# Weight low parts three chunks ahead and summed from HBM, with another order of the tiles in the recurrent branch

## The chip, the cores and the metric

The kernel runs on one core of one Trainium2 chip, in one launch. The metric is device time in microseconds, from the first to the last instruction of an execution; the number given for a kernel is the median of its runs. Engines are named as in the profile: PE (TensorE), DVE (VectorE), ACT (ScalarE), POOL (GpSimd), SP (SyncE, which here only issues transfers).

## The reference, cut to what matters

512 tokens of width 1024 go through two blocks, all in fp32. The first is a hybrid attention layer; the second is a layer run twice with its own weights (`l` = 0, 1).

```python
def hybrid_layer(x, ...):                    # first block, once
    proj = rms_norm(x) @ w_in                # q, three k/v pairs, gates, z, indexer ...
    kc, vc = compress(k), compress(v)        # silu(flat @ w1 + b1) @ w2 over blocks of 32
    o_nsa = g0 * compressed + g1 * selected + g2 * window      # 8 heads
    score = sum_h relu(qi @ ki) * wi         # indexer; top 128 keys of each query
    o_dsa = attention over the chosen keys   # 8 heads
    return x + concat(o_nsa * silu(z_n), o_dsa * silu(z_d)) @ w_out

def hybrid_layer_2(x, c, positions, ...):    # second block, for l in 0, 1
    mod = c @ w_ada + b_ada                  # 6 vectors: shift, scale, gate, twice
    h = rms_norm(x) * (1 + sc_m) + sh_m
    x_lru, q_down, kv_down, k_rope, gate_a, gate_b = split(h @ w_in)
    y_a = rg_lru(causal_depthwise_conv(x_lru), positions, ...)   # gated linear scan over tokens
    y_b = mla(q_down, kv_down, k_rope, ...)  # 8 heads of latent attention
    x = x + g_m * ((sigmoid(gate_a) * y_a + sigmoid(gate_b) * y_b) @ w_out)
    h = rms_norm(x) * (1 + sc_f) + sh_f
    gate, up = split(h @ w_ffn_in)
    return x + g_f * ((silu(gate) * up) @ w_ffn_out)
# and a last rms_norm
```

## The kernel before

**Products.** Every large product is made of three on TensorE. A weight tile of 128 x up to 1024 (a *chunk*) comes from HBM as `raw`; ACT rounds it to the matmul's format, `wh`; `wl` is what the rounding left over, raw - wh. The activations are split alike into `hh` and `hl`, and the product is hh·wh + hl·wh + hh·wl: 24 matmuls of 512 columns for a chunk. So a chunk can't be finished before its `wl` is there.

**Chunks.** `plan` lists all chunks in the order of their use, each with an engine for its low part. `load_chunk` (L172) issues the load on SP. `split_chunk` (L185) makes `wh` on ACT and then `wl` in one of two ways. With `DV`, DVE subtracts. With `GP`, ACT writes -raw to `wl`, and POOL issues a DMA that adds `raw`, from SBUF, to it (L203; the two together give raw less what the first copy rounded to). `run_ahead` (L211) splits up to `ahead[0]` chunks beyond the one in use, two in most places, and loads a chunk further; `take` (L221) hands a chunk to the code that multiplies. `raw`, `wh` and `wl` are rings of three buffers each. The `raw` of a chunk is free when all that reads it is done, in a GP chunk its accumulating DMA too.

**Order.** Code written as generators runs beside the matmuls: `go` starts one, `tick` and `pe` step all of them as matmuls are issued, `finish` runs one to its end. So the place of an evacuation or a split among the instructions of its engine follows from how much matmul work was written before it. `order(...)` names the engines that keep the written order strictly.

**Stages.** Times are of the profiled execution. *Projections* (6 to 206 us): the groups E, kv, C, A, Bq, Dv and z of `w_in`; beside C and A stand the compress steps (`cmp_step`), whose weights `cw1` are chunks of the plan too; `post_scores` and `best_keys` make the indexer's scores and, by rounds of MAX8 and MATCH_REPLACE8 on DVE, the mask of the top keys. *Attention* (216 to 366): units of 128 queries; beside them `ada_first(8)` makes a part of layer 0's `mod` from 16 tiles `ada` of 256 KB, one DVE product each. *First output* (366 to 418): eight chunks of `wo1`; `ada_first(0)` with 16 more tiles stands here. *Entry* of a layer (`enter`): norm and the first two input tiles; it also sums `shift` times the raw weights on DVE (`shifts`), which is why these chunks keep `raw` longer. *Branch* (layer 0: 440 to 612): four chunks of the latent vectors `lat`, then eight input tiles (conv, gates by `small_gates` on the split conv output `xch`/`xcl`, scan in `recur`), eight `gate_a` tiles and eight `gate_b` tiles, with `uqr` and `uqk`, the query weights of the latent attention. *Latent attention* `mla`, *wo2*, *feed-forward* (`ffi`, `ffo`; layer 0: 745 to 1100), then the same for layer 1, and the output. The 160 `ada` tiles of layer 0's other vectors and of layer 1 are loaded beside all this (L1859) and multiplied on DVE.

The branch before goes by pairs: gate_a, small gates, gate_a, scan, two gate_b, then the next pair's two input tiles. The first head of `mla` begins at the last pair's gate_b tiles, behind that pair's `recur`.

## Time and profile before

| | us |
|---|---|
| median of 3 runs | 1773.9 (1771.15 to 1777.37) |
| profiled execution, time | 1770.8 |
| profiled execution, span | 1769.0 |
| PE busy | 1687.9 (95%) |
| DVE busy | 1103.6 (62%) |
| ACT busy | 958.2 (54%) |
| POOL busy | 381.1 (22%) |
| granted TensorE clock, mean | 0.986 |
| DMA | 235.91 MB, 133 GB/s |

The share of an engine is a mean over stages with different limits. TensorE's row is the one to start from: what it isn't busy, and what it is busy at a lower clock, is all that can be won without leaving matmuls out. For every other engine a busy share matters only where TensorE's waits name it.

### The profile page before, as it was taken

How to read it: one execution, taken by the hardware profiler on the slowest of the kernel's cores; microseconds unless marked ns; L12 is line 12 of the kernel's file. 1: busy time of each engine (PE TensorE's matmuls, PEld its weight loads, DVE VectorE, ACT ScalarE, POOL GpSimd, SP SyncE). 2: the span in 40 equal slices, each digit the busy share in tenths (PEclk: the TensorE clock that was granted, in tenths of full speed). 3: DMA queues.
4: the chain of work that ended last, by engine and by line, in shares of the span. 5: the costliest groups of instructions: out<-in, count | busy, mean ns of one | idle time of the engine just before them, and what ended most of it. 6: DMA issues, size and time to landing. Idle time of an engine off the chain costs nothing.

```text
span 1769.0 us, 22764 instructions
## 1 busy us (share of the span) xinstructions
PE 1687.9 (95%) x8122; PEld 1389.5 (79%) x8124; DVE 1103.6 (62%) x2048; ACT 958.2 (54%) x1729; POOL 381.1 (22%) x429
## 2 busy tenths in 40 slices
PE   6979899989998999999999999999999999999998
PEld 5868677667776788888888888887788888888887
DVE  5767788768689876746555546657676733333335
ACT  5558787975766786442222224887885532222223
POOL 3236344531225244100000000235243100000000
PEclk9989999999999999999999999999999999999999
DMA  6546643165787822366457443564422343333322
GB/s 199 148 125 140 150 108 84 48 177 134 189 256 209 236 49 70 98 184 226 155 190 236 149 132 94 146 146 126 124 60 72 97 129 96 96 95 98 100 86 74
DMA packets 84976, 235.91 MB, mean 133 GB/s; under 512 B 10368, under 2 KB 13056, under 8 KB 84864
## 3 DMA queue, kind: packets, MB, share of 16 engines
q1 hardware_dynamic: 73600, 194.82, 35.5%
q0 software_dynamic: 11264, 39.65, 12.1%
q8 instruction: 64, 1.05, 0.2%
q14 instruction: 48, 0.39, 0.1%
HBM read 192.69 MB, written 2.10 MB: 110 GB/s over the span
## 4 chain that ended last, share of the span: by engine, by line
PE 65%; DVE 10%; issue 9%; DMA 8%; ACT 6%; POOL 3%; SPq 0%; POOLq 0%; DVEq 0%; ACTq 0%
PE mm L84 38%; PE s L84 20%; PE o L84 3%; DMA wl<-raw 3%; DMA ada<-in_ada_dram 3%; DVE ada L1850 2%; DMA raw<-in_w_dram 2%; PE pt L930 1%; ACT p L71 1%; PE pt L2017 1%; PE pt L84 1%; DVE wl L74 1%; DVE xc L1534 1%; ACT L71 1%; DVE xl L1622 0%
## 5 line engine op out<-in xcount | busy, mean ns | idle before, releaser
L71 ACT ACTIVATE wh<-raw 128x1024 fp32r<-128x1024 f32 (+3 forms) x257 | 263.3, 1026 | 578.6 <-PE mm L84 361.7
L84 PE MATMUL mm<-hh,wh 128*128 128x512 f32 x1408 | 444.9, 393 | 3.6 <-DVE z L74 3.4
L84 PEld LDWEIGHTS mm<-hh,wh 128*128 128x128 f32 x1408 | 265.3, 189 | 58.4 <-DVE z L74 3.5
L84 PE MATMUL mm<-hh,wl 128*128 128x512 f32 x736 | 290.1, 394 | 4.6 <-DMA wl<-raw 4.5
L74 DVE TENSOR_TENSOR wl<-raw,wh 128x1024 fp32r<-128x1024 f32 (+3 forms) x179 | 213.8, 1196 | 115.9 <-ACT wh L71 113.5
L84 PE MATMUL s<-hh,wh 128*128 128x512 f32 x688 | 213.8, 390 | 0.0
L74 POOL TENSOR_TENSOR nv<-nv,pwr 128x4 f32<-128x4 f32 (+1 forms) x6 | 7.4, 1234 | 776.7 <-DVE nv L1321 432.7
L84 PEld LDWEIGHTS mm<-hh,wl 128*128 128x128 f32 x736 | 139.4, 189 | 35.3 <-DMA wl<-raw 6.5
L84 PEld LDWEIGHTS s<-hh,wh 128*128 128x128 f32 x688 | 129.4, 188 | 26.6
L84 PE MATMUL s<-hh,wl 128*128 128x512 f32 x352 | 137.8, 392 | 2.7 <-DMA wl<-raw 2.7
L84 PE MATMUL mm<-uh,wh 128*128 128x512 f32 (+1 forms) x364 | 139.2, 382 | 0.0
L84 PE MATMUL mm<-ul,wh 128*128 128x512 f32 (+1 forms) x364 | 139.0, 382 | 0.0
L84 PE MATMUL mm<-uh,wl 128*128 128x512 f32 (+1 forms) x364 | 139.0, 382 | 0.0
L203 POOL DMA_DIRECT2D wl<-raw x78 | 68.9, 887 | 254.4 <-ACT wl L71 214.8
L1850 DVE SCALAR_TENSOR_TENSOR ada<-ada,c_bc 128x512 f32<-128x512 f32 x160 | 115.8, 756 | 7.2 <-DMA ada<-in_ada_dram 7.2
L74 DVE TENSOR_TENSOR sg<-s,sg 128x512 f32<-128x512 f32 x42 | 29.1, 692 | 116.4 <-PE s L84 116.4
L71 ACT ACTIVATE p<-s,st 128x512 f32<-128x512 f32 (+3 forms) x160 | 83.9, 527 | 23.7 <-DVE st L1994 16.9
L1769 DVE SCALAR_TENSOR_TENSOR x<-mm,mod,x 128x512 f32<-128x512 f32 x46 | 34.5, 751 | 92.2 <-PE mm L84 92.2
L84 PEld LDWEIGHTS s<-hh,wl 128*128 128x128 f32 x352 | 66.4, 189 | 17.7 <-DMA wl<-raw 4.0
L84 PE MATMUL mm<-yh,wh 128*128 128x512 f32 x256 | 79.6, 392 | 0.3 <-DVE x L2119 0.3
L71 ACT ACTIVATE wl<-raw 128x1024 fp32r<-128x1024 f32 (+3 forms) x78 | 79.9, 1024 | 0.0
L84 PEld LDWEIGHTS mm<-uh,wl 128*128 128x128 f32 x364 | 68.4, 188 | 13.3
(430 smaller groups left out, 3640.7 us busy)
## 6 DMA issues: line engine op xcount, KB each, us to landing
ada<-in_ada_dram SPq DMA_DIRECT2D x192, 256.0 KB, 4.1
raw<-in_ffi_dram SPq DMA_DIRECT2D x88, 512.0 KB, 3.6
wl<-raw POOLq DMA_DIRECT2D x67, 512.0 KB, 5.4
raw<-in_w_dram SPq DMA_DIRECT2D x66, 512.0 KB, 3.9
raw<-in_ffo_dram SPq DMA_DIRECT2D x32, 512.0 KB, 3.7
raw<-in_wo_dram SPq DMA_DIRECT2D x24, 512.0 KB, 3.7
raw<-in_ffo_dram SPq DMA_DIRECT2D x16, 384.0 KB, 3.2
x<-in_xT_dram SPq DMA_DIRECT2D x16, 256.0 KB, 4.9
```

Of the source, the lines that this page charges most:

```text
L71: nc.scalar.activation(o, i, f, **kw)
L74: (e or nc.vector).tensor_tensor(o, x, y, op)
L84: nc.tensor.matmul(o, l, r, start=start, stop=stop)
L203: nc.gpsimd.dma_start(lo[:, :n].bitcast(F32), raw[:, :n], accum_op=ALU.add)
L930: nc.tensor.transpose(tp[:n, r * 128:(r + 1) * 128], srcs[r], ident)
L1534: nc.vector.scalar_tensor_tensor(xc[:, d:], x_[:, :S - d], vec[:, j * 8 + m:j * 8 + m + 1], xc[:, d:], ALU.mult, ALU.add)
L1769: nc.vector.scalar_tensor_tensor(x[m], ps, mod[:, 40 + m:41 + m], x[m], ALU.mult, ALU.add)
L1850: nc.vector.scalar_tensor_tensor(w, w, 1.0, c_bc[:, hf * 512:(hf + 1) * 512], ALU.mult, ALU.mult, accum_out=parts[l][:, j, hf:hf + 1])
L2017: nc.tensor.transpose(tp[:, kb * 128:(kb + 1) * 128], p[:, kb * 128:(kb + 1) * 128], ident)
```

## The change

- *Splitting.* `split_chunk` becomes `low_first` and `high`. `low_first` makes ACT's -raw and issues the accumulation, three chunks ahead (`ahead` 3); `high` makes `wh` two chunks ahead; loads go four ahead. The accumulating DMA reads the chunk from HBM again instead of from `raw`. The rings are now `raw` 2, `wh` 3, `wl` 4.
- *Who makes the low part.* More chunks are GP: the accumulating DMAs grow from 78 to 125, the 1024-wide DVE subtractions shrink from 153 to 111. All of C, A, Bq, Dv, the branch, `uqr`, `uqk`, `wo2` and the first five `ffi` chunks are GP; two E chunks are subtracted on POOL; the other `ffi` chunks and `ffo` stay on DVE.
- *Compress weights.* `cw1` leaves the plan; `load_cw` puts it into two tiles of the `ada` ring, half a step each, after the step before has been issued.
- *Shift sums.* The sums of `shifts` move from `enter` into `low_first`.
- *Branch order.* A table `STEPS` sets it: the next pair's input tiles (X) come before the gate_b tiles (B), and the first head's projections (L) before the last scan (R6).
- *Modulation.* `ada_both` runs `ada_first(8)` and `ada_first(0)` beside the attention.
- *End of the projections.* The stage ends when the mask of the third group of queries exists; the fourth is finished by the first unit that needs it. Its scores lie in a tile of their own.
- *Small ones.* x loads of the start are contiguous, E's third chunk is loaded behind them; the tile `isres` goes (the test stands in the operation that used it); ten attention tiles `p` become nine. ACT's table loads grow from 45 to 57.

```diff
-    def split_chunk(i):
+    def low_first(i):
+        n, e = plan[i][3:]
+        while count[0] <= i:
+            load_chunk()
+        raw = loaded[i]
+        if e is GP:
+            lo = lows[i] = wpool.tile([128, 1024], F32R, tag="wl", name=name("wl"), bufs=LB)
+            act(lo[:, :n], raw[:, :n], scale=-1.0)
+            yield 1
+            nc.gpsimd.dma_start(lo[:, :n], source(i), accum_op=ALU.add)
...
-            nc.gpsimd.dma_start(lo[:, :n].bitcast(F32), raw[:, :n], accum_op=ALU.add)
...
+    def high(i):
...
+        if e is GP:
+            ready[i] = h, lows.pop(i), raw
+            act(h[:, :n], raw[:, :n])
             return
...
-    ahead = [2]
+    ahead = [3]
...
-        while count[1] <= min(i + ahead[0], len(plan) - 1):
-            k = count[1]
+        end = len(plan) - 1
+        while count[3] <= min(i + ahead[0] - 1, end):
+            k = count[3]
+            if count[1] <= k:
+                count[1] += 1
+                yield from low_first(k)
+            count[3] += 1
+            yield from high(k)
+        while count[1] <= min(i + ahead[0], end):
             count[1] += 1
-            yield from split_chunk(k)
-        if count[0] <= i + 3:
+            yield from low_first(count[1] - 1)
+        while count[0] <= min(i + ahead[0] + 1, end):
             load_chunk()
...
+    STEPS = [(s_[0], int(s_[1])) for s_ in """
+        A0 S0 S1 A1 R0 X2 X3 B0 T0 B1
+        A2 S2 S3 A3 R2 X4 X5 B2 Q0 B3
+        A4 S4 S5 A5 R4 X6 X7 B4 B5
+        A6 S6 S7 A7 L0 R6 B6 B7
+        """.split()]
...
-    while procs:
+    while any(p not in keys_p for p in procs):
         tick()
+    while 2 not in masks:
+        step(keys_p[0])
...
-    zs, more, ad = z_steps(), after_first(), ada_first(8)
+    def ada_both():
+        yield from ada_first(8)
+        yield from ada_first(0)
+
+    zs, more, ad = z_steps(), after_first(), ada_both()
```

On ACT, in layer 0's branch, this is the stretch from the first pair's last operations to the second pair's conv output. `gb` is a gate_b tile, `xl` and `xc` are an input tile and its conv, `xch` its high part, `wh`/`wl` the two copies of a chunk. Before:

```order
L71 ACTIVATE gb_4953<-mm 128x512
L71 ACTIVATE wh_4959<-raw_4921 128x1024
L71 ACTIVATE wl_4960<-raw_4921 128x1024
L71 ACT_TABLE_LOAD
L71 ACTIVATE gb_4900<-gb_4900 128x512
L71 ACTIVATE xl_4993<-mm 128x512
L71 ACTIVATE wh_5004<-raw_4967 128x1024
L71 ACTIVATE xc_4995<-xl_4993,vec_3910 128x512
L71 ACTIVATE wl_5005<-raw_4967 128x1024
L71 ACTIVATE gb_4953<-gb_4953 128x512
L71 ACTIVATE wh_5053<-raw_5013 128x1024
L71 ACTIVATE xch_5029<-xc_4995 128x512
```

And after the change:

```order
L74 ACTIVATE wh_4898<-raw_4808 128x1024
L74 ACTIVATE xc_4890<-xl_4888,vec_3982 128x512
L74 ACTIVATE wl_4900<-raw_4854 128x1024
L74 ACT_TABLE_LOAD
L74 ACTIVATE ri_4777<-ri_4777 128x512
L74 ACTIVATE ri_4791<-ri_4791 128x512
L74 ACTIVATE xl_4947<-mm 128x512
L74 ACTIVATE wh_4958<-raw_4854 128x1024
L74 ACTIVATE xc_4949<-xl_4947,vec_3982 128x512
L74 ACTIVATE wl_4960<-raw_4909 128x1024
L74 ACTIVATE xch_4931<-xc_4890 128x512
L74 ACTIVATE gb_4999<-mm 128x512
```

The input tiles and their convs now stand ahead of both gate_b tiles, and the two copies of a chunk have parted: `wl` of a chunk stands a tile ahead of its own `wh`.

On DVE, around the first head of `mla` in layer 0: `qkl` are the low parts of the first head's k and q, which its scores need; `ri` and the scan that writes `xl` belong to the last pair's `recur`. Before:

```order
L1611 SCALAR_TENSOR_TENSOR ri_5840<-a_5936,ri_5840 128x512
L74 TENSOR_TENSOR ri_5840<-ri_5840,isres 128x512
L1850 SCALAR_TENSOR_TENSOR ada_5906,part<-ada_5906,c_bc 128x512
L1850 SCALAR_TENSOR_TENSOR ada_5974,part<-ada_5974,c_bc 128x512
L1968 SCALAR_TENSOR_TENSOR qkl_5978<-s,qkh_5977 128x512
L1850 SCALAR_TENSOR_TENSOR ada_6002,part<-ada_6002,c_bc 128x512
L77 TENSOR_TENSOR qkl_5986<-s,qkh_5985 128x512
```

And after the change:

```order
L2011 SCALAR_TENSOR_TENSOR qkl_5956<-s,qkh_5955 128x512
L1893 SCALAR_TENSOR_TENSOR ada_5903,part<-ada_5903,c_bc 128x512
L80 TENSOR_TENSOR qkl_5964<-s,qkh_5963 128x512
L1893 SCALAR_TENSOR_TENSOR ada_5915,part<-ada_5915,c_bc 128x512
L1893 SCALAR_TENSOR_TENSOR ada_5943,part<-ada_5943,c_bc 128x512
L1656 SCALAR_TENSOR_TENSOR ri_5859<-a_5984,ri_5859 128x512
L1657 SCALAR_TENSOR_TENSOR ri_5859<-nres,ri_5859 128x512
```

The head's two low parts moved ahead of the whole of the last `recur`; products of modulation tiles still stand between them.

On SP, the loads around the end of the attention: `raw` of `in_wo` are the chunks of the first output, `ada` the modulation tiles, `x` the residual. Before:

```order
L179 DMA raw_3937<-in_wo_dram 128x1024
L284 DMA x_3900<-in_xT_dram 128x512 x4
L179 DMA raw_3968<-in_wo_dram 128x1024
L1183 DMA posi<-in_pos_dram 128x4
L1185 DMA posr<-in_posr_dram 128x512
L1187 DMA invf<-in_invf_dram 128x32
L1189 DMA vec_3910<-in_vec_dram 128x67
L1189 DMA vec_3911<-in_vec_dram 128x67
L1190 DMA fgain<-in_fgain_dram 128x8
L1064 DMA ada_3943<-in_ada_dram 128x512
L1064 DMA ada_3951<-in_ada_dram 128x512
L284 DMA x_3990<-in_xT_dram 128x512 x3
```

And after the change:

```order
L1126 DMA ada_3851<-in_ada_dram 128x512
L1509 DMA gw_4533<-in_lwa_dram 128x512
L1509 DMA gw_4599<-in_lwx_dram 128x512
L1248 DMA posi<-in_pos_dram 128x4
L1250 DMA posr<-in_posr_dram 128x512
L1252 DMA invf<-in_invf_dram 128x32
L1254 DMA vec_3982<-in_vec_dram 128x67
L1254 DMA vec_3983<-in_vec_dram 128x67
L1255 DMA fgain<-in_fgain_dram 128x8
L321 DMA x_4045<-in_xT_dram 128x512 x4
L194 DMA raw_4013<-in_wo_dram 128x1024
L194 DMA raw_4036<-in_wo_dram 128x1024
```

All modulation tiles of `ada_first` are now loaded before the tables, and between them and the following chunks of `wo` no more of them stand.

## Rows read from the trace of the kernel before

**Rows 1.** The page: busy time and share of TensorE, with its count of instructions

```profile
PE 1687.9 (95%) x8122; PEld 1389.5 (79%) x8124; DVE 1103.6 (62%) x2048; ACT 958.2 (54%) x1729; POOL 381.1 (22%) x429
```

**Rows 2.** Waits of TensorE: line, what it waited for, us in total, times, longest

```profile
PE mm L84 <- DMA wl<-raw: 24.0, 10, 4.8
...
PE pt L513 <- ACT R L71: 6.2, 2, 5.0
PE s L84 <- ACT xch L71: 4.0, 2, 3.0
PE pt L84 <- DMA wl<-raw: 3.7, 1, 3.7
PE s L84 <- DVE qkl L77: 3.6, 1, 3.6
PE mm L84 <- DVE z L74: 3.4, 1, 3.4
PE s L84 <- DMA wl<-raw: 2.7, 3, 1.3
PE pt L1648 <- DVE lat L1500: 2.2, 2, 1.2
...
PE s L84 <- DVE xcl L77: 1.7, 2, 1.6
PE pt L2017 <- POOL p L2000: 1.7, 1, 1.7
```

**Rows 3.** Windows: length, busy PE, PEld, DVE, ACT, POOL, clock, DMA share, GB/s

```profile
17.50:20.90 3.40, 3.22 (x12) 3.22 (x13) 3.09 (x5) 1.88 (x4) 3.07 (x3) 0.53 0.62 186
...
sum 23.80, PE 21.17 PEld 17.69 DVE 18.98 ACT 14.14 POOL 9.74; mean PE 3.53 PEld 2.95 DVE 3.16 ACT 2.36 POOL 1.62
...
195.00:201.80 6.80, 6.21 (x15) 4.91 (x16) 6.59 (x14) 1.55 (x3) 0.86 (x1) 0.51 1.01 217
611.50:618.30 6.80, 6.14 (x17) 4.71 (x18) 5.43 (x10) 3.69 (x6) 0.86 (x1) 0.52 0.83 205
```

**Rows 4.** The same view by stage: projections' end, attention, layer 0's branch, feed-forward

```profile
140.00:206.00 66.00, 60.16 (x289) 49.72 (x288) 58.69 (x111) 53.68 (x144) 35.45 (x41) 0.95 0.65 151
216.00:366.00 150.00, 144.26 (x835) 106.28 (x836) 119.59 (x282) 126.18 (x323) 73.46 (x99) 1.00 0.29 73
...
440.00:612.00 172.00, 156.12 (x677) 126.90 (x677) 138.31 (x243) 122.75 (x181) 57.11 (x46) 0.98 0.77 220
...
800.00:1090.00 290.00, 290.00 (x1281) 240.23 (x1280) 164.03 (x304) 79.94 (x99) 0.00 (x0) 1.00 0.55 174
```

**Rows 5.** Groups by shape: count | busy us, mean ns of one | idle before, releaser

```profile
L71 ACT ACTIVATE wh<-raw 128x1024 fp32r<-128x1024 f32 x220 | 232.3, 1058 | 530.6 <-PE mm L84 340.4 <-issue 138.7 <-PE s L84 26.7
L74 DVE TENSOR_TENSOR wl<-raw,wh 128x1024 fp32r<-128x1024 f32 x153 | 189.5, 1239 | 109.6 <-ACT wh L71 107.3
...
L71 ACT ACTIVATE wl<-raw 128x1024 fp32r<-128x1024 f32 x67 | 70.4, 1051 | 0.0
...
L71 ACT ACT_TABLE_LOAD x45 | 57.7, 1283 | 1.5 <-PEq L2254 0.7
...
L1058 DVE SCALAR_TENSOR_TENSOR ada<-ada,c_bc 128x512 f32<-128x512 f32 x32 | 22.9, 719 | 15.1 <-DMA ada<-in_ada_dram 15.0
```

**Rows 6.** The page: DMA queue (packets, MB, share) and issues (KB, us to landing)

```profile
q0 software_dynamic: 11264, 39.65, 12.1%
...
raw<-in_ffi_dram SPq DMA_DIRECT2D x88, 512.0 KB, 3.6
wl<-raw POOLq DMA_DIRECT2D x67, 512.0 KB, 5.4
```

**Rows 7.** Timeline of POOL in layer 0's branch: start, us, instruction

```profile
558.33 0.88 POOL L203 DMA_DIRECT2D wl<-raw  x1
```

**Rows 8.** Timeline of DVE at the end of the projections

```profile
194.13 0.68 DVE L602 MATCH_REPLACE8 sco<-m,sco 128x512 f32<-128x512 f32 x1
194.84 0.69 DVE L74 TENSOR_TENSOR z<-mm,rbx 128x512 f32<-128x512 f32 x1
```

More of the change, by code (lines that the diff above doesn't have):

```diff
@@ L30 @@
 AR = 4
+RB = 2
+HB = 3
+LB = 4
 TICK = 640.0
@@ L166, in wait, with shifts, source @@
             yield 1
-    plan = []
-    loaded, ready, count = {}, {}, [0, 0, 0]
+    plan, shift_of, shift_parts = [], {}, {}
+    loaded, lows, ready, count = {}, {}, {}, [0, 0, 0, 0]
+    def shifts(l, c0, i):
+        if i == 0:
+            shift_parts[l, c0] = pp.tile([128, 3, 128], F32, tag="wsh", name=name("wsh"), bufs=1)
+        return shift_parts[l, c0][:, i], mods[l][:, c0:c0 + 8]
+    def source(i):
+        key, l, o, n, _ = plan[i]
+        return (a[key] if l is None else a[key][l])[:, o:o + n]
     def load_chunk(beside=None):
@@ L183, in load_chunk @@
             count[0] += 1
-    def split_chunk(i):
+    def low_first(i):
[8 more added lines that the diff above has]
+            nc.gpsimd.dma_start(lo[:, :n], source(i), accum_op=ALU.add)
+            if i in shift_of:
+                by_k, shift = shifts(*shift_of[i])
+                for kt in range(KD):
+                    w_ = raw[:, kt * 128:(kt + 1) * 128]
+                    if kt == 0:
+                        nc.vector.tensor_scalar(by_k, w_, shift[:, 0:1], None, ALU.mult)
+                    else:
+                        nc.vector.scalar_tensor_tensor(by_k, w_, shift[:, kt:kt + 1], by_k, ALU.mult, ALU.add)
+                    if kt % 2:
+                        yield 1
@@ L1327, in rms, with enter @@
         yield rb
-    def enter(st, gain, shift, weights, pool):
+    def enter(st, gain, shift, part, weights, pool):
         hs, box = [], {"n": 0}
@@ L1381, in enter @@
         sh = pp.tile([128, 3], F32, tag="shw", name=name("shw"), bufs=2)
-        by_k = Lp.tile([128, 3, 128], F32, "F", name("wsh"))
-        def shifts(i):
-            for kt in range(KD):
-                raw = ws[i][2][:, kt * 128:(kt + 1) * 128]
-                if kt == 0:
-                    nc.vector.tensor_scalar(by_k[:, i], raw, shift[:, 0:1], None, ALU.mult)
-                else:
-                    nc.vector.scalar_tensor_tensor(by_k[:, i], raw, shift[:, kt:kt + 1], by_k[:, i], ALU.mult, ALU.add)
-                if kt % 2:
-                    yield 1
         def last(k):
@@ L1400, in enter @@
         for i in range(2):
-            ahead[0] = 2 - i
+            ahead[0] = 3
             ws.append(take(*weights[i]))
-            parts_.append(go(later(5, shifts(i))))
             w_dense(xg, ws[i], pss[i], 0, KD - 1, need=last)
@@ L1715, in layer @@
         order(mybir.EngineType.PE, mybir.EngineType.Activation)
-        hs, first, need = enter(st, sc1[:, 8:16], mod[:, 24:32], [("ffi", l, k * 1024, 1024) for k in range(3)], POOL_FF)
+        hs, first, need = enter(st, sc1[:, 8:16], mod[:, 24:32], (l, 24), [("ffi", l, k * 1024, 1024) for k in range(3)], POOL_FF)
         if l == 0:
@@ L2062, in mla @@
         yield
-        ahead[0] = 1
+        ahead[0] = 2
         yy = {}
```

200 lines of the change are left out of this document (97 added, 103 removed).

## The prediction, made before the changed kernel was run

> **What bounds the kernel now.** I read the page's busy times first: TensorE works 95% of the span [rows 1], so only TensorE's own lost time counts, and a busy DVE, ACT or DMA counts where TensorE waits for it. The view of waits on TensorE says what that lost time is [rows 2]. Three of its rows are waits for a low part, `wl<-raw`, still on its way through DMA: 24.0 + 3.7 + 2.7 = 30.4 us in 14 waits. Next come `R`, which the change leaves as it is, then `xch`, `xcl` and `lat` (the recurrent branch, 4.0 + 1.7 + 2.2), `qkl` and `p` (the first latent-attention head, 3.6 + 1.7) and `z` (end of the projections, 3.4). Then the granted clock: behind each of the longer waits TensorE runs at its 1.2 GHz level, half of 2.4, for 3.4 or 6.8 us. Six such stretches stand behind a wait for a low part and sum to 23.8 us (the first, at 17.5 us, with a clock of 0.53); one of 6.8 us stands behind `z`, one behind `qkl` [rows 3]. In the feed-forward part nothing is lost: 290.00 busy of 290 us, 1281 matmuls, so 0.226 us for each and 24 x 0.226 = 5.4 us for a weight chunk [rows 4]. What the change does there can cost but not gain.
>
> **What it removes.**
>
> A. Low parts. Today the low part of chunk n is begun two chunks before its use: an ACT copy of 1.05 us [rows 5], the issue on POOL of 0.88 us [rows 7], a landing of 5.4 us [rows 6], 7.3 us in all against 2 x 5.4 = 10.9 us of lead. That holds until something stands ahead of it. The row at 558.33 us is such a case: POOL issues a low part only when a run of products has ended, the last of them at 558.33 [rows 7], and one of the 14 waits follows. With three chunks of lead there are 16.3 us, so a delay up to 9 us is hidden instead of up to 3.6. No single wait of the 14 is above 4.8 us [rows 2], so nearly all should go. I take 27 of 30.4; ends 15 and 30.4.
>
> B. The clock behind those waits. 23.8 us at about half rate lose about 11.5 us of matmuls. If the waits go, so do these; I take 10.5, ends 5 and 11.5.
>
> C. Order in the branch. The next pair's input tiles now come before the gate tiles, so between a conv's input and the matmuls that read `xch` and `xcl` there are two more tiles, 11 us. The 5.7 us of those waits go, and the transposes of `lat` stand behind a gate tile (2.2). I take 7.5; ends 4 and 7.9.
>
> D. First head. Its projections now stand ahead of the last scan's gate tiles; two tiles, 11 us, lie between them and the scores, where one lay. 3.6 (`qkl`) + 1.7 (`p`) + 6.8 us at half rate = 3.3: 8.6. I take 8.5; ends 3 and 8.6.
>
> E. End of the projections. TensorE waits 3.4 us for `z`, which on DVE stands behind three rounds of the top-k search (the row of `z` at 194.84 follows one of their steps directly [rows 8]), and then loses 3.4 to the clock. The change ends this stage without waiting for the last search, but the order on DVE still has rounds ahead of each `z`, and DVE is busy 58.69 of these 66 us [rows 4]. So I take only 2; ends 0 and 6.8.
>
> Sum of the gains: 27 + 10.5 + 7.5 + 8.5 + 2 = 55.5 us.
>
> **What it adds.**
>
> F. The attention stage gets the first layer's 16 modulation products as well as those it had: 16 x 0.72 = 11.5 us of DVE [rows 5]. DVE works 119.59 of the 150 us there, TensorE 144.26 [rows 4]. 131 of 150 still fits, but softmax steps wait behind single products. Ends 0 and 11.5; I take 3, nearer to the lower end, since DVE has 30 us free there and TensorE only 6.
>
> G. DMA in the first layer's branch. More chunks there go the way over ACT and an accumulating DMA: two latent chunks, two gate-a and eight gate-b tiles, and one chunk each of `uqr` and `uqk`, 14 together. The software queue took 12.1% of 16 engines' 1769 us for 39.65 MB [rows 6], that is 214 us over 39.65/0.524 = 75.7 chunks, 2.83 us of all engines for one. The stage's share is 0.77 of 172 us, 132 us [rows 4]; with 14 x 2.83 = 40 it is 172, and the stage itself shall shrink from 172 to about 151 by A to D. So by this price the DMA engines are full there. Lower end 0: an accumulation that reads HBM may take less engine time than one that reads and writes SBUF, and its low parts have 9 us of slack. Upper end 172 - 151 = 21. I take 6, nearer to the lower end, because the share that a queue shows includes time in which its packets wait on one another.
>
> A rule of the Trainium skill stands against the new source: "DMA: Bandwidth & Descriptors", section "Where 436 GB/s comes from", has HBM to SBUF limited at about 358 GB/s and SBUF to SBUF at 435. By that figure the stage's 220 GB/s x 172 us = 37.8 MB plus 14 x 0.524 MB are 45.2 MB, an estimated 126 us, less than 151: G would be 0 and the sum 6 us lower. The row of the stage, a share of 0.77 at 220 GB/s, implies 286 GB/s when full, below the page's figure. No run here shows yet which holds for an accumulation from HBM.
>
> H. Start and compress. The third E chunk's load goes behind all x tiles (0 to 3 us). The compress weights leave the stream of chunks and are loaded into two small tiles just after the step before has read them: eight steps, each with a landing of 3.6 to 5.4 us [rows 6] against a chunk of 5.4 us, so 0 to about 1 us each. Together 0 to 11; I take 4, nearer the lower end as a compress step itself lasts over a microsecond and lies between.
>
> I. ACT. 47 more low copies at 1.05 and 12 more table loads at 1.28 us [rows 5] are 49 + 15 = 65 us. In the branch of the first layer that is some 22 us on 122.75 of 172 [rows 4]; ACT is then at 145 of 151 and becomes the next to be late. DVE loses 42 subtractions of 1.24 us [rows 5]. I take 2; ends 0 and 10.
>
> Nothing for the rest. Two raw buffers instead of three: in the feed-forward part a raw tile is held for its load (3.6), ACT's copy (1.06) and DVE's subtraction (1.24) [rows 5, 6], 5.9 us, and two buffers give 10.9 us for that. What hides it is 5 us of slack; if loads took 8 us there, each chunk would cost TensorE time. The shift sums (16 and 24 DVE operations for a layer's two entries) are only moved earlier. The accumulate needs the raw tile no longer, so a load waits for ACT's two copies alone.
>
> Sum of the costs: 3 + 6 + 4 + 2 = 15 us. Net 40.5. The profiled execution took 1770.8 us; 1770.8 - 40.5 = 1730.3, and the median of the runs stands 3.1 above that execution, so **1733 us**. With all gains at their upper end (65) and no cost it is 1709.
>
> **The rivals.**
>
> 1. The DMA engines are full in the first layer's branch. For it: the 172 us of G, and a DVE wait for modulation data there. Against it: layer two's branch has no such load, and the packets of an accumulate may overlap. It costs 21 in place of 6, and the low parts of this stage are late again (another 0 to 10): 1748 to 1762, with 1750 as its likeliest.
>
> 2. The change does not do what it says. The low parts are late because of POOL's queue and ACT's, not because they are begun late, and both queues get more work: 47 more issues on POOL. Then A and B bring nothing (37.5): 1770. For it is the row at 558.33 us; against it that the delay seen there is below the added lead.
>
> 3. Slower. An accumulation from HBM, with the loads of raw, wh and the modulation tiles on the same engines, lands later than three chunks can cover. With a ring of four and three in preparation, a chunk takes at least a third of landing L plus copy, issue and queueing (1.05 + 0.88 + about 1.5 = 3.4), so its wait is (L + 3.4)/3 - 5.4. About 80 chunks before the feed-forward parts go this way. The net gain of 40.5 us is used up at 0.5 us for each, and the kernel is measurably slower from 0.6: L = 3 x 6.0 - 3.4 = 14.6 us, where the landing from SBUF is 5.4 [rows 6]. At L = 16 each waits 1.07 us, +85: 1818 before other waits are hidden in it, about 1790 if half of them are.
>
> **How the numbers follow.** Forecast 0.63 (1712 to 1747), rival 1 0.20, rival 2 0.08, rival 3 0.09. To the low side the range reaches 1712, almost all gains at their ends; to the high side it takes in rival 1, to 1765. What is left out is rivals 2 and 3 and a little of the forecast, 0.2. A run of this kernel can tell 0.3%, 5.3 us, from no change. Faster by more than that (below 1768.6): forecast, rival 1 and a third of rival 2, 0.86. Within: most of the rest of rival 2, 0.05. Slower: rival 3, 0.09.
>
> **What would show it.** Right: no row of TensorE waiting for `wl` above 1 us between 60 and 620 us, and no stretch at half clock there (A, B); no waits for `xch`, `xcl`, `qkl` (C, D); the feed-forward stages still at full busy time. F would show as waits for softmax tiles in the attention, G as a DMA share near 1.0 in the first branch with late `wl` or raw, H as waits for `cw`, I as waits for an ACT result. The landing of the accumulates settles rival 3: below 10 us it is out. The forecast is wrong if new waits on TensorE take more than 15 us, or if the half-clock stretches stay although the waits shrink.

## The result and the profile after

The changed kernel takes 1787.1 us (median of 6 runs, 1782.23 to 1789.53) against 1771.8 us for the kernel before in 6 runs beside it: a ratio of 1.0081, 95% interval 1.0061 to 1.0101. It is slower by 0.8%; the forecast was 1733 us. The profiled execution of the changed kernel has a span of 1786.5 us, 17.5 more than before.

The page of the changed kernel: busy times, the queue of the accumulating DMAs (packets, MB, share), and two rows of issues (KB each, us to landing). They answer to [rows 1] and [rows 6].

```profile
PE 1696.1 (95%) x8124; PEld 1396.0 (78%) x8124; DVE 1049.1 (59%) x1998; ACT 1017.1 (57%) x1788; POOL 410.3 (23%) x478
...
q0 software_dynamic: 18032, 63.98, 21.3%
...
wl<-in_w_dram POOLq DMA_DIRECT2D x65, 512.0 KB, 6.6
...
wl<-in_wo_dram POOLq DMA_DIRECT2D x24, 512.0 KB, 6.8
```

TensorE's idle time is 90.4 us where it was 81.1, and its busy time is 8.2 us longer for the same matmuls, most of which is time at the lower clock (0.983 on the mean against 0.986). The low parts land 6.6 us after their issue instead of 5.4. The waits of TensorE (line, releaser, us in total, times, longest), to be laid beside [rows 2]:

```profile
PE s L87 <- ACT p L74: 8.9, 8, 4.0
PE mm L87 <- DMA wl<-in_w_dram: 7.2, 4, 2.7
...
PE mm L87 <- ACT gb L74: 6.2, 2, 3.5
PE pt L1693 <- DVE cl L1706: 5.7, 1, 5.7
PE mm L87 <- ACT ga L74: 5.5, 1, 5.5
...
PE o L87 <- DMA cw<-in_cw_dram: 3.1, 2, 1.7
PE s L87 <- ACT qkh L74: 2.9, 1, 2.9
...
PE mm L87 <- DMA wl<-in_wo_dram: 2.0, 1, 2.0
```

The waits for low parts did go: 7.2 + 2.0 and a last 0.5 instead of 30.4. `xch`, `xcl` and `z` are gone too. In their place stand results of ACT (`gb`, `ga`, `qkh`, `p`) and `cl`.

Where the time went is read from the timeline of TensorE, at the first matmul of each stage. "Sum" is the sum of squares `o<-ones,sa` at a layer's entry; a head starts at `s<-qkh,qkh`.

| stage | before, us | after, us | change |
|---|---|---|---|
| start to the first product of `ptl` with VA (projections) | 226.4 | 209.4 | -17.0 |
| attention, to first product of `wo1` | 142.0 | 156.5 | +14.5 |
| first output, to the first sum | 48.1 | 43.6 | -4.5 |
| layer 0: entry and branch, to the first head | 191.6 | 196.8 | +5.2 |
| layer 0: heads, to `wo2` | 73.5 | 85.0 | +11.5 |
| layer 0: `wo2`, to the second sum | 57.1 | 59.1 | +2.0 |
| layer 0: feed-forward, to the third sum | 362.5 | 364.6 | +2.1 |
| layer 1: entry to the fourth sum | 296.5 | 300.7 | +4.2 |
| layer 1: feed-forward and output | the same within 0.4 | | |

The projections are 17.0 us shorter (other executions of the same code there took 224.5 to 228.1 before and 205.3 to 209.4 after); seven of the 14 waits for low parts, 15.9 us, lay there. The attention gave most of it back: of its 14.5 us 8.5 are idle time of TensorE and 6.0 the same matmuls at a lower clock (0.97 on the mean against 1.00). Layer 0 from the first to the second sum, where A to D were to save some 20 us, grew from 322.2 to 340.9. The windows of that stage in the changed kernel (branch, then first heads; columns as in [rows 3]):

```profile
440.00:605.00 165.00, 145.25 (x626) 116.86 (x625) 108.72 (x209) 118.76 (x171) 54.30 (x51) 0.98 0.92 249
605.00:700.00 95.00, 81.19 (x482) 69.11 (x481) 68.65 (x157) 72.13 (x155) 37.91 (x53) 0.91 0.36 86
```

The DMA share of the branch rose from 0.77 to 0.92, and the heads behind it run at a mean clock of 0.91. What ACT and DVE waited for between the first two sums of the changed kernel:

```profile
ACT wl L74 <- DMA raw<-in_w_dram: 26.5, 10, 5.5
...
ACT wl L74 <- DMA raw<-in_uqk_dram: 7.5, 3, 4.7
```

```profile
DVE ada L1893 <- DMA ada<-in_ada_dram: 30.1, 12, 5.6
```

With the chunks of `wo` and `ffi` ACT's waits for raw make 40 us. Before, ACT waited 3.1 us for raw there and DVE 7.2 us for modulation tiles:

```profile
ACT wh L71 <- DMA raw<-in_w_dram: 3.1, 2, 2.0
```

```profile
DVE ada L1850 <- DMA ada<-in_ada_dram: 7.2, 5, 3.1
```

SP issues both kinds of load in one order, and it too stands longer at the modulation tiles, until DVE has freed a buffer for the next one, with the loads of raw behind it (the changed kernel, then the one before):

```profile
SPq L1902 <- DVE ada L1893: 92.1, 33, 8.2
```

```profile
SPq L1859 <- DVE ada L1850: 51.7, 34, 5.0
```

How this reaches TensorE shows in a stretch of the timeline (start, us, instruction, idle before and its releaser):

```profile
550.44 1.06 ACT L74 ACTIVATE wl<-raw 128x1024 fp32r<-128x1024 f32 x1 [3.12 <-DMA raw<-in_w_dram]
...
553.07 1.28 ACT L74 ACT_TABLE_LOAD   x1 [1.57 <-DVE ada L1893]
...
556.85 1.28 ACT L74 ACT_TABLE_LOAD   x1
...
558.14 0.60 ACT L74 ACTIVATE ga<-mm 128x512 f32<-128x512 f32 x1
...
558.79 1.22 PE L87 MATMUL mm<-hh,wh 128*128 128x512 f32 x2 [5.52 <-ACT ga L74]
```

ACT stands 3.12 us at the early copy for a low part, because its raw has not landed; then it waits for DVE, which is busy with modulation products; the evacuation of a gate tile comes behind all that, and TensorE needs the buffer that this tile leaves. The early copy, made to take the low part out of TensorE's way, now stands in ACT's.

### The profile page after: what moved, and what is told of

Read it like the earlier page. It is cut to its first block, busy times and chain, and to the rows that moved or that the text cites. A ratio compares the mean times of both kernels' runs of the same rounds, so it can differ in the third digit from the quotient of the medians.

```text
span 1786.5 us, 22790 instructions
## 1 busy us (share of the span) xinstructions
PE 1696.1 (95%) x8124; PEld 1396.0 (78%) x8124; DVE 1049.1 (59%) x1998; ACT 1017.1 (57%) x1788; POOL 410.3 (23%) x478
## 4 chain that ended last, share of the span: by engine, by line
PE 68%; DMA 8%; DVE 7%; ACT 6%; issue 6%; POOL 3%; SPq 0%; DVEq 0%; POOLq 0%; ACTq 0%
PE mm L87 42%; PE s L87 19%; PE o L87 3%; DMA ada<-in_ada_dram 3%; DMA raw<-in_w_dram 3%; DMA raw<-in_ffi_dram 1%; PE pt L992 1%; PE pt L2060 1%; DVE ada L1893 1%; ACT R L74 1%; ACT wl L74 1%; ACT wh L74 1%; DVE xc L1579 1%; PE pt L87 1%; DMA wl<-in_wo_dram 1%
## 5 line engine op out<-in xcount | busy, mean ns | idle before, releaser
L77 DVE TENSOR_TENSOR wl<-raw,wh 128x1024 fp32r<-128x1024 f32 (+2 forms) x130 | 152.7, 1175 | 114.1 <-ACT wh L74 111.8
L209 POOL DMA_DIRECT2D wl<-in_w_dram x81 | 71.1, 884 | 592.2 <-DVE wsh L217 331.4
L74 ACT ACTIVATE wl<-raw 128x1024 fp32r<-128x1024 f32 (+2 forms) x125 | 129.6, 1036 | 79.7 <-DMA raw<-in_w_dram 41.3
L1893 DVE SCALAR_TENSOR_TENSOR ada<-ada,c_bc 128x512 f32<-128x512 f32 x160 | 115.8, 755 | 30.4 <-DMA ada<-in_ada_dram 30.1
L74 ACT ACTIVATE p<-s,st 128x512 f32<-128x512 f32 (+3 forms) x160 | 84.0, 528 | 21.3 <-DVE st L2037 12.1
L87 PEld LDWEIGHTS mm<-uh,wh 128*128 128x128 f32 x364 | 68.4, 188 | 13.3
L87 PEld LDWEIGHTS mm<-ul,wh 128*128 128x128 f32 x364 | 68.4, 188 | 13.3
```

Source lines behind the costliest of these rows:

```text
L74: nc.scalar.activation(o, i, f, **kw)
L77: (e or nc.vector).tensor_tensor(o, x, y, op)
L87: nc.tensor.matmul(o, l, r, start=start, stop=stop)
L209: nc.gpsimd.dma_start(lo[:, :n], source(i), accum_op=ALU.add)
L1893: nc.vector.scalar_tensor_tensor(w, w, 1.0, c_bc[:, hf * 512:(hf + 1) * 512], ALU.mult, ALU.mult, accum_out=parts[l][:, j, hf:hf + 1])
```

## Experiments

Unless said otherwise the measure is the stage from the first to the second sum: 322.2 us before, 340.9 in the changed kernel. Ratios are to the kernel before, with 95% intervals. A stage is read from one execution: kernels with the same code there took 322.2 to 322.9 us with the old code and 340.8 to 345.3 with the changed one, so a few us between two kernels say little.

**Is it the number of accumulations?** Fourteen chunks of a branch go back to DVE:

```diff
-                w2_(16 + m)
+                w2_(16 + m, DV)
...
-                chunks("uqr", l, 0, 1024, 1, GP)
+                chunks("uqr", l, 0, 1024, 1, DV)
```

(and likewise two latent chunks, two gate_a tiles and the first `uqk` chunk.)

> The changed kernel with one thing undone: in both layers' branches the low parts of two latent chunks, two gate_a and eight gate_b tiles, uqr and the first uqk chunk are subtracted on DVE again, as before the change. Measure: layer 0's stage from the row sum of squares (o<-ones,sa) ahead of it to the next one, 322.3 us before the change, 340.9 after. Theory 1 (the DMA engines are full, share 0.92; raw comes late, and ACT, whose -raw copy stands first in its order, holds everything behind it): 14 accumulations fewer are some 40 us of engine time, so the share falls to about 0.75, ACT's waits for raw in the branch from 33 to under 10 us, and the stage to 325 or less; the whole kernel gains 12 to 18 us. Theory 2 (two raw buffers are too few): the loads still wait for ACT's second copy, the stage stays above 335. Theory 3 (the new order of tiles): above 335 too.

Measured: 1787.1 us, 1.0086 (1.0063 to 1.0110), no gain; the stage takes 336.4. Its DMA share fell, from 0.69 over the stage of the changed kernel to 0.57, about that of the kernel before (0.56), yet ACT still waits 29.6 us for raw and DVE 28.0 us for modulation tiles, and TensorE now waits for DVE's own low parts:

```profile
PE mm L87 <- DVE wl L77: 11.5, 3, 5.2
```

So a full set of DMA engines, as rival 1 had it, isn't the whole cause. How much it is of it this run can't tell, because these new waits may hide what the lighter traffic gave.

**Is it the order of tiles?** The old order in the changed kernel (but for the first head's projections, L0, half of which stood ahead of B6 before):

```diff
-        A0 S0 S1 A1 R0 X2 X3 B0 T0 B1
-        A2 S2 S3 A3 R2 X4 X5 B2 Q0 B3
-        A4 S4 S5 A5 R4 X6 X7 B4 B5
-        A6 S6 S7 A7 L0 R6 B6 B7
+        A0 S0 S1 A1 T0 R0 B0 B1 X2 X3
+        A2 S2 S3 A3 R2 B2 B3 X4 X5 Q0
+        A4 S4 S5 A5 R4 B4 X6 X7 B5
+        A6 S6 S7 A7 R6 B6 L0 B7
```

> The changed kernel with the old order of the tiles in the branch (gate_b tiles of a pair ahead of the next pair's input tiles, first head behind the last scan) and all else as changed. Theory 3 (the new order costs): the stage from sum to sum falls from 340.9 towards 325, the total by 10 to 18 us. Theory 1 (DMA full) and theory 2 (two raw buffers): the share stays near 0.92, ACT still waits 25 us or more for raw in the branch, and the stage stays at 335 to 350; it may be longer by the waits for xch, xcl and qkl (up to 15 us) which the order was to remove.

Measured: 1791.3 us, 1.0108 (1.0079 to 1.0136); the stage takes 342.3. The branch to the first head is 212.7 instead of 196.8, the heads 70.7 instead of 85.0. The new order moves some 15 us of waiting from the branch into the heads. In layer 1, which has no modulation loads beside its branch, the old order is the slower one: 307.3 from entry to the fourth sum, where the kernels with the new order and the same code take 298.8 to 304.1.

**The modulation tiles.** 64 tiles of 256 KB are loaded beside layer 0's branch on the same SP queue as raw. Four kernels leave out all or a part of that. Without loads and products, in the changed kernel and in the one before (the sums that the products would make are set to zero once, so that part of `mod` is left out):

```diff
         for j in range(j0, j1):
             for hf in range(2):
+                if l == 0:
+                    yield every
+                    continue
```

> The changed kernel without the 64 modulation tiles of layer 0 that are loaded and multiplied beside its branch (16.8 MB and some 48 us of DVE; that part of mod stays as it is after its bias). Theory 1: 16.8 MB fewer take the DMA share in the branch from 0.92 to about 0.65, ACT's waits for raw from 33 to under 8 us, the stage from 340.9 to 322 or less, total 15 to 22 us less. Theory 2: raw still waits for a free buffer; ACT's waits stay above 20 us and the stage above 332. Theory 3: the same as theory 2, but DVE's own waits for modulation data (30 us) go, which may give up to 8 us.

> The kernel before without the same 64 modulation tiles, as the base for the run above. All theories: its stage of 322.3 us has only one long low-part wait and one DVE wait that come from DMA, so it gains 3 to 10 us; theory 1 wants the gain clearly smaller here than in the changed kernel, theories 2 and 3 want about the same in both.

Then the products without the loads (here the products are of `c` with itself):

```diff
-            nc.vector.scalar_tensor_tensor(w, w, 1.0, c_bc[:, hf * 512:(hf + 1) * 512], ALU.mult, ALU.mult,
+            ch = c_bc[:, hf * 512:(hf + 1) * 512]
+            nc.vector.scalar_tensor_tensor(w, w if l else ch, 1.0, ch, ALU.mult, ALU.mult,
...
-                nc.sync.dma_start(w, a["ada"][l, :, j * D + hf * 512:j * D + (hf + 1) * 512])
+                if l:
+                    nc.sync.dma_start(w, a["ada"][l, :, j * D + hf * 512:j * D + (hf + 1) * 512])
```

And loads and products without the dependence: the loads stay, and the product neither reads nor writes the loaded tile (`sp_` is a tile of its own):

```diff
-            nc.vector.scalar_tensor_tensor(w, w, 1.0, c_bc[:, hf * 512:(hf + 1) * 512], ALU.mult, ALU.mult,
+            ch = c_bc[:, hf * 512:(hf + 1) * 512]
+            nc.vector.scalar_tensor_tensor(w if l else sp_, w if l else ch, 1.0, ch, ALU.mult, ALU.mult,
```

> The changed kernel without the 64 loads of modulation tiles beside layer 0's branch, but with their 64 DVE products (each of c with itself, so that part of mod is other data). The kernel without both had a stage of 302.5 us between the first two sums of squares, the changed kernel 340.9. Theory A (the late tiles: DVE, in order, stands at a product whose tile has not landed, and holds conv, xcl, qkl and the softmax sums behind it; or their loads take the engines): stage 303 to 312. Theory B (the 48 us of DVE time themselves): 325 to 340.

> The changed kernel with the same 64 loads and the same 64 products, but the products no longer read the tiles that were loaded (they are of c with itself), so the traffic stays and DVE never waits for it. If the in-order wait on DVE is what costs, the stage falls from 340.9 to 305 to 318, with a DMA share near 0.9. If the traffic itself (engines full, raw and low parts late) is, it stays above 330 though DVE waits for no tile.

| kernel | total, us | stage, us |
|---|---|---|
| changed | 1787.1 | 340.9 |
| changed, products don't read the loaded tiles | 1781.3 | 331.7 |
| changed, no loads | 1761.5 | 312.0 |
| changed, neither loads nor products | 1745.4 | 302.5 |
| before | 1771.8 | 322.2 |
| before, neither loads nor products | 1754.4 | 304.4 |

The stage in the three kernels that leave something out of the changed one, in that order (columns as in [rows 3]):

```profile
404.90:736.60 331.70, 303.24 (x1472) 251.20 (x1471) 225.42 (x448) 234.89 (x389) 110.20 (x122) 0.97 0.70 179
```

```profile
405.50:717.50 312.00, 297.21 (x1472) 248.57 (x1472) 226.03 (x448) 236.82 (x391) 113.98 (x122) 0.99 0.62 137
```

```profile
406.10:708.60 302.50, 293.39 (x1472) 246.01 (x1472) 173.96 (x317) 234.92 (x390) 111.27 (x122) 1.00 0.61 141
```

The 64 tiles cost the changed kernel 38.4 us (340.9 - 302.5), the kernel before only 17.8 (322.2 - 304.4). Of the 38.4, 9.2 go when DVE no longer stands in order behind a tile that has not landed, 19.7 more when the loads are gone, and 9.5 with the products. The first of these is the least certain: the profiled execution was the fastest of that kernel's seven, and by the medians of the whole kernels the three steps are 5.8, 19.9 and 16.0. Without the tiles the changed branch is as good as the old one, 302.5 against 304.4. So the change and these loads hinder each other, and about half of the cost is the loads being there at all: raw in this stage lands after a median of 5.7 us in the changed kernel, 3.9 before, and 4.5 in the changed kernel without the loads. Whether that is the engines' bandwidth or the place in SP's one queue isn't told apart by these runs.

The old kernel without the tiles shows something else. These are the longest waits of its TensorE in the stage:

```profile
PE pt L84 <- DMA wl<-raw: 2.8, 1, 2.8
PE pt L1649 <- DVE lat L1501: 2.1, 2, 1.2
PE mm L84 <- DMA wl<-raw: 1.3, 1, 1.3
PE s L84 <- ACT p L71: 1.1, 1, 1.1
```

The waits for `xch`, `xcl` and `qkl` [rows 2], 9.3 us, are gone here, though the order of tiles is the old one. They were a cost of the modulation tiles, not of the order alone.

**Two raw buffers.** Three of them, paid for by smaller rings elsewhere (in the attention too, so that only layer 0 counts; the ring R of the second block shrinks as well, and layer 1, which has it too, takes 300.3 against 300.7):

```diff
-RB = 2
+RB = 3
...
-    P = HP(pP, {"R": 3, "cp": 4})
+    P = HP(pP, {"R": 2, "cp": 3})
...
-           {"p": 9, "pth": 3, "ptl": 3, "pc": 2, "st": 5})
+           {"p": 7, "pth": 3, "ptl": 3, "pc": 2, "st": 5})
...
-    Lp = HP(ctx.enter_context(tc.tile_pool(name="block2", bufs=1, reuse_waits="tile")), {"R": 20, "PT": 4, "G": 16, "F": FB, "qr": 1})
+    Lp = HP(ctx.enter_context(tc.tile_pool(name="block2", bufs=1, reuse_waits="tile")), {"R": 18, "PT": 4, "G": 16, "F": FB, "qr": 1})
```

> The changed kernel with three raw buffers instead of two; the room comes from smaller rings elsewhere (R 3 to 2 and cp 4 to 3 in the projections, p 9 to 7 in the attention, R 20 to 18 in the second block), so only the branch of layer 0 is to be compared. The last runs put theory 1 (DMA engines full) in doubt: with a share of 0.67 the modulation tiles were as late as with 0.92. Theory 2, now with its size: with two buffers a load may start only when ACT has made wh of the chunk two before, and on ACT the next low copy follows one chunk (5.4 us) later, while copy and landing take 1 + 5 us; so ACT waits at that copy, and SP, waiting for the buffer, holds the modulation tiles queued behind the load. With three buffers ACT's waits for raw in the stage between the first two sums of squares (340.9 us) fall from 40 to under 10 us, DVE's for modulation data from 30 to under 12, and the stage to 315 to 325. Theory 1: the share stays near 0.9 and so do the waits; stage above 335.

Measured: the stage takes 340.0, though ACT's waits for raw fell from 40 us to 4.4, and DVE's for modulation tiles grew from 30.1 to 41.1:

```profile
ACT wl L74 <- DMA raw<-in_w_dram: 4.4, 2, 4.2
```

```profile
DVE ada L1893 <- DMA ada<-in_ada_dram: 41.1, 13, 8.5
```

The wait moved to DVE and the modulation tiles, and TensorE lost as much as ever. (1802.3 us in total, most of the added time in the attention, 175.9 us with seven p tiles.)

**The source of the accumulation.** Two chunks of lead for the low part and one for wh, rings of three, once from HBM and once from SBUF, all else as changed (the edit from one to the other; its `.bitcast(F32)` on the target was not tried apart, here and in the next run):

```diff
-            nc.gpsimd.dma_start(lo[:, :n], source(i), accum_op=ALU.add)
+            nc.gpsimd.dma_start(lo[:, :n].bitcast(F32), raw[:, :n], accum_op=ALU.add)
```

> The changed kernel with low parts two chunks ahead, wh one ahead, loads three ahead and rings of three raw, three wh and three wl (the early places of ahead as before the change); source of the accumulation, order and engines as changed. Theory 2 (two raw buffers): the stage between the first two sums of squares falls from 340.9 to 320 to 330, ACT's waits for raw there under 15 us, while waits of TensorE for wl come back in the projections (10 to 20 us). Theory 1 (DMA full): same traffic, so the stage stays above 335.

> The run a_two with one difference: the accumulating DMA reads the chunk from SBUF (raw) again instead of from HBM. If the source matters (theory 1, HBM traffic), the landing of wl falls from 6.6 to about 5.4 us, the DMA share in layer 0's branch falls by 0.05 or more, and the stage is at least 8 us shorter than in a_two. If it doesn't, the stage differs by less than 5 us; raw is held longer by the landing, so it may even be longer.

Measured: 1808.9 us (1.0194, 1.0169 to 1.0220) from HBM, 1784.8 (1.0058, 1.0040 to 1.0077) from SBUF: 24 us. Not in the stage, where it was looked for and where they differ by 2.7 the other way (336.3 and 339.0), but up to the first sum (397.6 and 389.3) and behind the second. The stage is as long here as with three chunks of lead, though ACT hardly waits for raw with three buffers of it; DVE waits 40.6 and 39.9 us for modulation tiles. The reverse edit, SBUF to HBM, alone in the kernel before:

> The kernel before with one part of the change: the accumulating DMA reads the chunk from HBM instead of from raw in SBUF (rings, order and leads as before). From the two runs with two chunks of lead, where the source from HBM was 24 us slower: a median of 1778 to 1795, landing of wl 5.4 to 6.5 or more, engine time per chunk 2.83 to about 3.1 us, more waits of TensorE for wl. If the source costs only under the other rings, it is within 5 us of the kernel before; if it relieves SBUF, it is faster.

Measured: 1789.1 us, 1.0099 (1.0084 to 1.0114). This one line costs 16 us there. Its queue, landing and waits of TensorE:

```profile
q0 software_dynamic: 11264, 39.65, 12.2%
...
wl<-in_w_dram POOLq DMA_DIRECT2D x41, 512.0 KB, 7.6
```

```profile
PE mm L84 <- DMA wl<-in_w_dram: 28.0, 17, 4.7
PE s L84 <- DMA wl<-in_ffi_dram: 6.9, 4, 3.7
PE pt L84 <- DMA wl<-in_w_dram: 6.0, 1, 6.0
...
PE mm L84 <- DMA wl<-in_wo_dram: 5.5, 1, 5.5
...
PE s L84 <- DMA wl<-in_w_dram: 1.0, 1, 1.0
```

The engines are busy for as long as before (12.2% against 12.1% [rows 6]); what grew is the landing, 7.6 against 5.4 us, and TensorE waits 47.4 us for low parts instead of 30.4. The third chunk of lead in the changed kernel has to make up for that first.

**The attention.** One group of modulation tiles back behind it; the whole search in the projections again; and, in the kernel before, nine p tiles, and both groups in the attention:

```diff
-    zs, more, ad = z_steps(), after_first(), ada_both()
+    zs, more, ad = z_steps(), after_first(), ada_first(8)
...
-    jobs = [go(tables())]
+    jobs = [go(tables()), go(ada_first(0, 1))]
```

> The changed kernel with the second group of 16 modulation tiles back behind the attention. From the first product with VA to the first of the output weights the attention takes 156.5 us in the changed kernel, 142.0 in the one before. Theory 4 (the 16 added DVE products and their waits on the in-order DVE): it falls to 142 to 147 and the next stage grows from 43.6 to 46 to 48. Theory 5 (rounds of the top-k search left over into the attention) and theory 6 (nine p tiles instead of ten): it stays above 152.

> The changed kernel with the whole top-k search finished inside the projections again, as before the change. If the left-over rounds are what lengthens the attention beyond the 10 us of the modulation products (theory 5), the attention falls from 156.5 to 150 to 153 and the stage of the projections grows by no more than 3; if not (nine p tiles, or softmax waits of another kind), the attention stays above 154.

> The kernel before with nine attention tiles p instead of ten, nothing else. In the changed kernel the attention takes 156.5 us from the first product with VA to the first of the output weights, 142.0 before; 10 of the 14 follow the 16 modulation products, the left-over search rounds give nothing, and with seven tiles (a_ring3) it took 175.9. If the ninth-tile limit is the rest, the attention here takes 145 to 149 and the whole kernel 3 to 6 us more. If not, 141 to 143, and the rest stays open.

> The kernel before with one part of the change: both groups of 16 modulation tiles beside the attention. If the 16 products cost in the attention what they give back behind it, the attention goes from 142.0 to 150 to 154, the next stage from 48.1 to 38 to 41, and the whole kernel stays within 4 us. If the freed DMA time behind the attention also brings the low parts there in time, it gains 4 to 8 us.

| kernel | attention, us | first output, us | total, us |
|---|---|---|---|
| before | 142.0 | 48.1 | 1771.8 |
| changed | 156.5 | 43.6 | 1787.1 |
| changed, one group back | 146.3 | 53.0 | 1786.0 |
| changed, search finished before | 156.5 | 43.8 | 1791.7 |
| before, nine p tiles | 144.4 | 45.6 | 1774.4 |
| before, both groups beside the attention | 152.3 | 44.5 | 1778.0 |

The 16 products cost 10 us in the attention and give 4 to 9 back behind it; alone they make the kernel before 1.0029 times as long (1.0013 to 1.0046). Nine tiles cost 2.4 there and return it in the next stage. The left-over search rounds cost nothing in the attention. Some 2 of its 14.5 us stay open.

**A version that beats both.** First block as changed, but low parts two chunks ahead from SBUF with rings of three; second block's order and division between DVE and DMA as before. The first try made wh only one chunk ahead, because the changed `run_ahead` makes it a chunk later than the low part:

> What looks best of both: the first block as in the run a_two_sbuf (changed order of loads, compress weights beside, modulation tiles in the attention, all GP, but low parts two ahead from SBUF, rings of three), the second block's order of tiles and its division between DVE and DMA as before the change. If the stages add up, the first sum of squares comes at about 389 us (416.5 before) and the rest takes as long as before: 1743 to 1752. If the gain of the first block is given back in the branch, whose modulation loads then meet other traffic, 1760 to 1772.

Measured: 1774.2 us, 1.0016 (0.9998 to 1.0035). The first sum comes at 390.0, 26.5 us early, and all of that is lost later; TensorE waits for DVE's low parts, which are begun one chunk ahead:

```profile
PE mm L87 <- DMA wl<-raw: 18.5, 11, 2.9
PE mm L87 <- DVE wl L77: 17.3, 9, 4.1
```

With wh two ahead:

```diff
-        while count[3] <= min(i + ahead[0] - 1, end):
+        while count[3] <= min(i + ahead[0], end):
```

> As c_mix, with wh (and with it DVE's subtraction) two chunks ahead instead of one, which is what the kernel before does: the first block with the changed order of loads, compress weights beside, all GP and the modulation tiles in the attention; low parts two ahead from SBUF, rings of three; the second block's order and division as before. In c_mix TensorE waited 19.7 us for DVE's wl, which was begun one chunk ahead. If that was all, those waits go, the first sum of squares stays at 388 to 392 (416.5 before), the stages behind it take 322, 362, 297 as before, and the median is 1744 to 1752. If the first block's gain came from wh being later (less on ACT), that sum comes at 396 to 405 and the median is 1755 to 1762.

Measured: **1761.1 us, 0.9927 (0.9910 to 0.9943)**, faster than both. The stage is 322.2 as before:

```profile
393.90:716.10 322.20, 301.62 (x1473) 249.93 (x1472) 244.41 (x467) 217.64 (x371) 102.50 (x103) 0.98 0.56 156
```

The first sum comes at 393.9, 22.6 us early, and the whole profiled execution is 11.1 us shorter. The rest is lost behind the second sum, in stages that were to stay as they were; one wait of 2.9 us for a low part stands there, and most of it isn't explained. On this base, the new order of tiles alone, and one group of modulation tiles back behind the attention:

> The run c_mix2 with one difference, the changed order of tiles in both branches (next pair's input tiles ahead of gate_b, first head ahead of the last scan). If the order does what it was for, without the later loads, the waits for xch, xcl, qkl and p (about 11 us) and a stretch at half clock go: the stage between the first two sums is 8 to 16 us shorter than in c_mix2. If the order itself is bad (theory 3), it is 5 us or more longer. If the waits only change their names, within 4 us.

> The run c_mix2 (1761.1, 0.9927 of the kernel before) with the second group of 16 modulation tiles back behind the attention. From the kernel before with both groups in the attention (+10.3 us there, -3.6 in the next stage, median 1.0029): the attention falls from 154.2 to 144 to 147, the next stage grows from 43.6 to 46 to 48, the first sum of squares comes at 386 to 390 instead of 393.9 and the median is 1755 to 1758. If the two groups cancel as in the changed kernel (156.5 + 43.6 against 146.3 + 53.0), within 2 us of c_mix2.

Measured: with the new order 1765.8 us, 0.9959 (0.9943 to 0.9976); layer 0's stage is 6.4 us longer than in c_mix2 and layer 1's 0.9 shorter. With one group back 1765.7, 0.9952 (0.9931 to 0.9972), where the first sum comes at 393.0 and the groups cancel within a microsecond, as in the changed kernel. This kernel has c_mix2's code in layer 0, and the stage took 325.2; so the loss by the order, 328.6 against 322.2 and 325.2, is small and not clear of what one execution can tell. A gain it is not, though ACT never waits for raw here: DVE's wait for modulation tiles is 16.1 us with the new order, 8.3 in c_mix2.

## Why the prediction was wrong

*What bounds the kernel* held. TensorE's lost time is the measure, and the whole loss of 17.5 us is found in its waits and its clock.

*A and B* (low parts and the clock behind them) were right for what they remove: 30.4 us became 9.7, and the projections, where seven of those waits lay, are 17 us shorter. But the working took the landing of 5.4 us from [rows 6], which is a landing from SBUF, for the new source. From HBM it is 6.6 here and 7.6 in b_hbm, and the source alone costs 16 us at the old lead. Part of the added lead bought nothing but that. And the clock that was lost behind these waits is lost behind others now: its mean is 0.983, before 0.986.

**The step that failed is the price of layer 0's branch.** G counted the branch's traffic as time of the DMA engines, 6 us, and "Nothing for the rest" let a load wait "for ACT's two copies alone". The 64 modulation tiles, which share SP's queue with raw and DVE's order with the branch, got no price of their own; beyond their part in the DMA share they were in the text as a clause each of rivals 1 and 3. The runs show in its place that these tiles cost 38.4 us in the changed kernel and 17.8 before. The difference, 20.6, covers the 18.7 us by which the stage grew, and without the tiles the two kernels are even (302.5 and 304.4). How it divides between the engines' bandwidth, SP's queue and DVE's order stays open. No single part of the change makes it: it stays with the old order (342.3), the old division (336.4), three raw buffers (340.0), and two chunks of lead with either source (336.3 and 339.0), and is gone in c_mix2 (322.2), which takes all of these back.

The slack of the two raw buffers is one link of it. It was worked out for the feed-forward part, where it held, and not for the branch. There the low copy stands three chunks ahead on ACT, the load for it may start only after ACT has made wh of the chunk two before, and raw took 5.7 us to land against 5.4 for a chunk. ACT waited 40 us at that copy, with every evacuation behind it. The prediction asked what is queued behind the low part's DMA on POOL, and not what would be queued behind the copy that comes before it on ACT. But the third buffer took this wait away and the stage stayed as long, with DVE's wait for modulation tiles at 41.1 us.

*G and rival 1* pointed to the right stage; but rival 1 still counted on the gains of A to D there, and its mechanism was only half right: with 14 accumulations fewer, and the DMA share of the old kernel, the stage stays at 336.4. (Its upper end is 1758 by its own terms, 1733 + 15 + 10, not 1762.) The rule of the Trainium skill in "DMA: Bandwidth & Descriptors", "Where 436 GB/s comes from" would have made G nothing at about 358 GB/s. The branch ran at 249 GB/s with a share of 0.92, 271 GB/s when full, so that ceiling was not what was met.

*C and D* (16 us forecast) brought nothing in layer 0. They put the waits for `xch`, `xcl` and `qkl` down to the order of tiles, but the old kernel loses these waits when the modulation tiles go, with its order unchanged. In the changed kernel they are gone but for 0.5 us, and those for `gb`, `cl`, `ga` and `qkh` came, 20.3 us, more than the 15 that the prediction named as the sign of being wrong. The tiles between producer and consumer were counted, not the evacuations and DVE products that the order puts between them on ACT and DVE.

*E* came about as taken: the wait of 3.4 us for `z` is gone, one of 2.7 us for `p` came in its place, and one stretch of 3.4 us at half clock is left there where one of 6.8 stood. *F* was the right mechanism with a wrong size: 3 taken, 10 measured, near its upper end, of which 4 to 9 come back in the next stage. DVE's spare 30 us were no help; that softmax steps wait behind single products in DVE's fixed order, as the prediction has it, is likely but was not shown apart. *H*: 3.1 us of waits for `cw` against 4 taken. *I* (2 taken, ends 0 and 10) is the term into which ACT's lateness would have fallen. It was priced as busy time, which grew by 21.9 us in the stage, as reckoned (22). That alone costs little: without the modulation tiles ACT has the same work (234.9 us) and the stage takes 302.5.

*Rival 3* had the right sign and a mechanism of which the first half is true, a later landing from HBM. Its threshold of 14.6 us was not met and isn't what decided: at a landing of 6.6 us TensorE waits only 9.7 us for low parts in all, and the time is lost elsewhere, in layer 0's branch and the attention. *Rival 2* is out: the waits went.

## What to carry to other kernels

Where engines keep the written order, an operation that is begun earlier stands earlier in the order of every engine it uses, and each of these engines then waits for its inputs with all its other work behind it; price the earliest of its steps (here a copy on ACT that needs a loaded tile), not the last. When a buffer is given up to pay for lead, work out the time from its release to its next use in each stage, not only in the one with the largest traffic. And test a shared queue by taking its other user away, in the old kernel too: here each part of the change showed little in layer 0's stage when it was undone alone, and the other user showed the whole loss.

## What the runs showed of the hardware

An accumulating DMA of 512 KB from HBM takes the engines no longer than one from SBUF (12.2% and 12.1% of the span for the same bytes in b_hbm and the kernel before, 20.2% and 19.9% in a_two and a_two_sbuf) but lands later: 7.6 against 5.4 us in the first pair, 7.2 against 5.8 in the second (medians of the largest groups of 512 KB), although the chunk was loaded from the same place a few microseconds before.
